# Modulation chunks summed in one PSUM bank per batch, and an eleventh weight block, in a hybrid-then-MoE kernel

## The chip, the core and the metric

The kernel runs on one core of one Trainium2 chip. Its time is device time in microseconds (us), the median of three runs; the profile is one more execution, taken with the hardware profiler. TensorE is called PE in the profile's rows, VectorE DVE, ScalarE ACT, GpSimd POOL and SyncE SP. Nearly all loads are issued from SP's queue, which takes its instructions in order.

## The reference, cut to what matters

A block of two hybrid layers is followed by a block of two layers, each a mixer (neighbourhood attention, then grouped-query attention) and a mixture of 32 experts. All is fp32, with 256 tokens and D = 1024.

```python
c_act = jax.nn.silu(c)                                   # (1, 1024)
for i in range(DEPTH):                                   # 2 layers
    mod = c_act @ ada_w[i] + ada_b[i]                    # (1, 6 * 1024)
    sh1, sc1, g1, sh2, sc2, g2 = jnp.split(mod[:, None, :], 6, axis=-1)
    h = x * (1 + sc1) + sh1
    y = neighbourhood_mixer(h, ...) if i % 2 == 0 else gqa_mixer(h, ...)
    x = layer_norm(ALPHA * x + (1 + g1) * y, ...)
    h = x * (1 + sc2) + sh2
    y = hierarchical_moe(h, ...)   # sum of gate * (silu(h @ w_gate) * (h @ w_up)) @ w_down
    x = layer_norm(ALPHA * x + (1 + g2) * y, ...)
```

The part the change touches is `mod`: a vector of 2 x 6144 numbers from 24 weight chunks of 1024 x 512, of which each is 2 MB. An expert has 6 MB of weights: two gate_up halves and one down matrix of 2 MB each.

## The kernel before

**Weight blocks.** All large weights pass through blocks of 2 MB (`block`, 128 partitions of 16 KB). Eight (0 to 7) exist from the start, 8, 9 and 10 from the end of the hybrid layers on. A list, `ring`, says which block the next load takes: `chunk` pops its first entry and appends it again, so a load waits until the block's former content has been used. In the hybrid layers and the neighbourhood layer the ring is 0, 1, 2, 7; blocks 3 and 4 hold the weights' split into a high and a low part (`splitter`), 5 the transposed input, 6 the attention output, and 8, 9, 10 the queries, keys, values and scores. At an expert stage (`moe`) the ring is lengthened (L991): by 8, 9, 10, 3, 4, 5 in the first stage, by 7, 8, 9, 10, 3, 4, 5 in the second. Between the stages `role` renames the ten blocks in the order in which the first stage lets go of them, and the GQA layer uses 0, 1, 2 as its ring and 7, 9 and then 7, 2 for modulation chunks.

**Order of work.** The kernel is written as one stream of operations over tiles. A scheduler simulates it when the program is built and fixes the order on each engine and on SP's queue: the program's order is a priority, and an operation that is ready in the simulation may pass one that is not.

**Modulation chunks.** `ada_steps` (L724) yields the 24 chunks in two steps each, the load and the use; `ada()` takes as many steps at a place as `ADA_PLAN` (L28) says. So chunks 0 to 7 are loaded in the hybrid layers, 8 to 15 in the neighbourhood layer, 16 to 23 in the GQA layer. 22 chunks go over PE (`ada_cols`, L688): the condition vector stands 32 times side by side as the weight (`cact`), and 16 matmuls of 256 columns work in four groups of 32 PE columns into the one bank with the tag `pf`; the result is copied to `parts`, and a tail, run after the next chunk, turns it into four columns by two matmuls with two columns each (`sel`) and adds the bias into `modc`. Chunks 2 and 10 are stored transposed and go over DVE: four products with the condition row `crow` (L698), each with a sum along the row. The warm-up matmuls (`warm`) use the `pf` bank too.

**An expert stage** takes 16 pairs of experts: for a pair four gate_up loads and two down loads, the matmuls of the hidden layer, those of the down matrix and a scatter into the output that is held in four banks. After pair 8 there is a conditional part for experts with more than 32 tokens.

Of the kernel before, what the change touches and what calls it, by code (L numbers as in the profile page):

```python
# [7 lines left out]
F32 = mybir.dt.float32  # L8
# [3 lines left out]
OP = mybir.AluOpType  # L12
# [5 lines left out]
    0, 128, 256, 384, 768, 792, 824, 952, 956, 964, 966, 973)  # L18
# [8 lines left out]
ADA_ROWS = [int(i) for i in '001000000010000000000000']  # L27
# [4 lines left out]
def tile_hybrid_then_moe(ctx: ExitStack, tc: tile.TileContext, p: dict, out: bass.AP):  # L32
# [65 lines left out]
    def carve(b, *shapes):  # L98
        o, vs = 0, []
        for sh in shapes:  # L100
            n = 1
            for d in sh:
                n *= d
            v = b[:, o:o + n]
            o += n
            names = "abcde"[:len(sh)]
            if len(sh) > 1:
                v = v.rearrange(f"p ({' '.join(names)}) -> p {' '.join(names)}", **dict(zip(names[1:], sh[1:])))
            vs.append(v)
        return vs  # L110
# [41 lines left out]
    sel = cst[:, C_SEL:C_SEL + 2]  # L152
# [76 lines left out]
    def start(tmp):  # L229
# [19 lines left out]
        nc.sync.dma_start(crow, p["c_2"].partition_broadcast(128))  # L249
        th, csil = carve(tmp, (256,), (8,))  # L250
        for i in range(4):
            c = crow[:, i * 256:i * 256 + 256]
            S.activation(th, c, AF.Tanh, scale=0.5)
            V.tensor_scalar(th, th, 0.5, 0.5, op0=OP.mult, op1=OP.add)
            V.tensor_tensor(c, c, th, OP.mult)
# [3 lines left out]
        V.tensor_copy(cact, csil[:, :, None].to_broadcast([128, 8, 32]))  # L259

    cact = const.tile([128, 8, 32], F32, name="cact")
    crow = const.tile([128, D], F32, name="crow")
# [157 lines left out]
    def hybrid(l, w1, split, start=None):  # L420
# [256 lines left out]
        ada()  # L677

# [4 lines left out]
    pend = []  # L683

    def flush():
        while pend:
            pend.pop()()

    def ada_cols(l, sec, c, n):
        b0 = K_ADA + (l * 6 + sec) * 8 + c * 4  # L690
        o, b, one = modc[:, l, sec, c * 4:c * 4 + 4], col[:, b0:b0 + 4], 0.0 if sec in (0, 3) else 1.0
        w = chunk(adab[0] and adab[0]())
        nc.sync.dma_start(w, p["ada_w_2"][n])
        yield
        if ADA_ROWS[n]:
            w = w.rearrange("p (j k) -> p j k", j=4)
            for j in range(4):
                V.scalar_tensor_tensor(w[:, j], w[:, j], 1.0, crow, op0=OP.mult, op1=OP.mult, accum_out=o[:, j:j + 1])  # L698
            V.scalar_tensor_tensor(o, o, one, b, op0=OP.add, op1=OP.add)
            flush()  # L700
            yield
            return
        w = w.rearrange("p (k f) -> p k f", k=8)
        part = parts[:, c * 256:c * 256 + 256]
        first, ps = pin[0], PF()
        for k in range(4):
            for q in range(4):
                kk, f0 = q % 2 * 4 + k, q // 2 * 256
                i = mm(ps[32 * q:32 * q + 32, 0:256], cact[:, kk], w[:, kk, f0:f0 + 256], k == 0, k == 3)
                if first and k == q == 0:  # L710
                    tc.keep_in_program_order(i)
        evac(part, ps[:, 0:256])
        flush()

        def tail():
            ps = PF()
            for i in range(2):
                a = part[:, i * 128:i * 128 + 128]
                mm(ps[:, 2 * i:2 * i + 2], a, sel, True, True)
            V.scalar_tensor_tensor(o.rearrange("p (a i) -> p a i", i=2), ps[:, 0:4].rearrange("p (i a) -> p a i", i=2),  # L720
                                   one, b.rearrange("p (a i) -> p a i", i=2), op0=OP.add, op1=OP.add)

        pend.append(tail)
        yield  # L724

    def ada_steps():
        for n in range(24):
            yield from ada_cols(n // 12, n // 2 % 6, n % 2, n)
# [6 lines left out]
    def ada(n=None):  # L735
        for _ in range(next(plan) if n is None else n):
            next(steps, None)
# [252 lines left out]
    def moe(l, w1, lg, fs, fb, new):  # L990
        ring.extend(new)  # L991
# [263 lines left out]
    blocks(ctx.enter_context(pool("bigB", side="right")), range(8, 11))  # L1255
    w1 = ctx.enter_context(pool("misc"))
    for l in range(2):
        if l == 0:
            nxt = na_layer(l, split)
            adab[0] = None  # L1260
        else:
            role.update(zip((0, 7, 10, 8, 3, 4, 5, 1, 9, 2), ring))
            ring[:] = [0, 1, 2]
            adab[0] = cyc([7, 9])
            split = splitter()
            nxt = gqa_layer(l, split)
        moe(l, w1, *nxt, ([] if l == 0 else [7]) + [8, 9, 10, 3, 4, 5])


def _consts():  # L1270
# [11 lines left out]
    c[:, C_SEL:C_SEL + 2] = (i[:, None] % 32 == 0) & (i[:, None] // 64 == np.arange(2))  # L1282
# [17 lines left out]
def _layout(inp):  # L1300
# [16 lines left out]
    a["c_2"] = np.ascontiguousarray(g["c_2"][0])  # L1317
# [5 lines left out]
    for n in range(24):  # L1323
        l, s, c = n // 12, n // 2 % 6, n % 2
        w = g["ada_w_2"][l, :, s * D + c * 512:s * D + c * 512 + 512]
        if ADA_ROWS[n]:
            w = w.T.reshape(4, 128, D).transpose(1, 0, 2)
        else:
            w = w.reshape(8, 128, 512).transpose(1, 0, 2)
        a["ada_w_2"][n] = w.reshape(128, 4 * D)  # L1330
# [52 lines left out]
```

## Time and profile before

| | us |
|---|---|
| median of three runs | 1541.78 (1540.99 to 1545.21) |
| the profiled execution, its own time | 1540.82 |
| its span, first to last instruction | 1537.7 |
| PE busy | 1221.9 (79%) |
| DVE busy | 585.8 (38%) |
| ACT busy | 355.9 (23%) |

DMA moved 532.75 MB in the span. By the rows, the hybrid layers end at about 309 us, the first expert stage runs from about 480 to 926, the GQA layer from there to about 1083, and the second expert stage to the end. The row groups below are cited by number. A window's row gives the busy time of each engine in that stretch; a waits row says who waited for whom; SP's rows give the time at which loads are issued, not when they land. A matmul on fp32 data stands in the trace as two records.

### The profile page before, as it was taken

The numbers are of one execution on the slowest core, as the hardware profiler recorded it, in microseconds if no ns is written. First come the engines' busy times: TensorE is split into PE (matmuls) and PEld (weight loads), VectorE is DVE, ScalarE is ACT, GpSimd is POOL, SyncE is SP. The second block draws the span as 40 slices with busy tenths as digits, with TensorE's granted clock in tenths as the row PEclk, the third lists the DMA queues.
The fourth block names the chain that finished last, engine by engine and source line by source line (L and its number), as shares of the span: only waits on it lengthen the run. The fifth ranks groups of instructions, "written<-read, shape, count | busy, mean of one in ns | idle before, by whom it ended". The sixth has DMA issues, their size and how long they took to land.

```text
span 1537.7 us, 24637 instructions
## 1 busy us (share of the span) xinstructions
PE 1221.9 (79%) x10584; PEld 788.6 (51%) x10584; DVE 585.8 (38%) x1434; ACT 355.9 (23%) x759; POOL 48.1 (3%) x83
## 2 busy tenths in 40 slices
PE   6999899999998976674976767998897764686775
PEld 6897788787866432322432325757443321233322
DVE  6886687566575210100110116878311100011103
ACT  6454444435441100000100004472000000010000
POOL 0000000000000200000000000000300000000000
PEclk9999899999999998876998888999899877899798
DMA  9546553676487999999999997766999999999995
GB/s 368 192 174 263 219 191 117 262 280 254 183 339 317 425 428 428 426 427 425 427 427 426 427 425 326 291 276 250 378 428 428 427 427 427 426 427 427 427 428 214
DMA packets 46704, 532.75 MB, mean 346 GB/s; under 512 B 7040, under 2 KB 10240, under 8 KB 15104
## 3 DMA queue, kind: packets, MB, share of 16 engines
q1 hardware_dynamic: 45440, 527.99, 83.5%
q10 hardware_dynamic: 1152, 3.15, 0.5%
q8 instruction: 85, 1.39, 0.4%
q14 instruction: 27, 0.22, 0.0%
HBM read 530.07 MB, written 1.05 MB: 345 GB/s over the span
## 4 chain that ended last, share of the span: by engine, by line
DMA 46%; PE 43%; DVE 8%; ACT 2%; issue 1%; SPq 0%; DVEq 0%; ACTq 0%
DMA b<-in_moe_w_gate_up_dram 25%; DMA b<-in_moe_w_down_dram 19%; PE ps L159 13%; PE pd L174 11%; PE ps L174 11%; PE pd L159 3%; PE pf L159 2%; PE ps L156 2%; DVE b L125 2%; DMA b<-in_na_bias_dram 1%; ACT b L124 1%; DMA b<-in_ada_w_dram 1%; DMA b<-in_w_in_dram 0%; DVE b L217 0%; DVE mx L349 0%
## 5 line engine op out<-in xcount | busy, mean ns | idle before, releaser
L159 PE MATMUL ps<-b,b 128*32 128x256 f32 (+2 forms) x5248 | 484.0, 475 | 193.3 <-DMA b<-in_moe_w_gate_up_dram 129.5
L159 PEld LDWEIGHTS ps<-b,b 128*32 128x32 f32 (+1 forms) x5248 | 193.7, 120 | 426.2 <-issue 269.6
L174 PE MATMUL pd<-b,b 128*128 128x256 f32 (+2 forms) x1152 | 189.7, 322 | 8.0 <-DVE b L468 3.9
L174 PE MATMUL ps<-b,b 128*128 128x256 f32 (+1 forms) x1464 | 194.9, 292 | 0.8 <-DVE ch L217 0.5
L174 PEld LDWEIGHTS ps<-b,b 128*128 128x128 f32 x1464 | 183.8, 192 | 9.0 <-issue 3.6
L174 PEld LDWEIGHTS pd<-b,b 128*128 128x128 f32 x1152 | 163.5, 198 | 29.2 <-DVE b L468 5.9
L125 DVE TENSOR_TENSOR b<-b,b 128x1024 fp32r<-128x1024 f32 (+1 forms) x124 | 148.6, 1207 | 65.9 <-ACT b L124 64.6
L124 ACT CAST b<-b 128x1024 fp32r<-128x1024 f32 (+1 forms) x124 | 126.3, 1035 | 156.6 <-PE ps L174 70.0
L223 ACT COPY b<-ps 128x256 f32<-128x256 f32 (+1 forms) x81 | 36.0, 448 | 445.6 <-PE ps L159 298.8
L217 DVE COPY b<-ps 128x256 f32<-128x256 f32 (+1 forms) x71 | 36.0, 507 | 260.6 <-PE ps L159 216.6
L1096 DVE SCALAR_TENSOR_TENSOR sl<-sl,ps 128x128 f32<-128x128 f32 x64 | 18.4, 287 | 231.7 <-ACT sl L1095 231.7
L156 PE MATMUL ps<-cst,b 128*128 128x128 f32 (+1 forms) x404 | 75.3, 293 | 37.4 <-DVE b L217 17.4
L156 PEld LDWEIGHTS ps<-cst,b 128*128 128x128 f32 (+1 forms) x404 | 43.0, 141 | 102.4 <-DVE b L217 34.4
L159 PE MATMUL pd<-b 64*128 64x512 f32 (+1 forms) x384 | 83.1, 551 | 14.6 <-DVE b L1144 11.3
L1144 DVE TENSOR_TENSOR b<-ps,parts 128x512 f32<-128x512 f32 x32 | 22.1, 691 | 174.5 <-PE ps L159 173.7
L159 PEld LDWEIGHTS ps<-b,x 128*128 128x128 f32 x512 | 69.8, 222 | 26.2 <-issue 21.9
L159 PE MATMUL ps<-b,x 128*128 128x128 f32 x512 | 73.6, 309 | 9.2 <-PEq L1168 6.3
L1095 ACT ACTIVATE sl<-ps 128x128 f32<-128x128 f32 x64 | 17.7, 277 | 237.1 <-PE ps L156 237.1
L1114 POOL TENSOR_TENSOR b<-b,g 128x128 f32<-128x128 f32 x64 | 23.5, 399 | 1277.0 <-DVE b L1110 728.4
L159 PEld LDWEIGHTS pd<-b 64*128 64x128 f32 x384 | 34.7, 190 | 52.0 <-issue 24.3
L227 ACT ACTIVATE b<-ps,modc 128x128 f32<-128x128 f32 x64 | 29.0, 457 | 130.7 <-DVE b L221 77.5
L221 DVE TENSOR_SCALAR b<-ps,modc 128x128 f32<-128x128 f32 x64 | 25.8, 408 | 80.1 <-ACT b L227 41.9
(294 smaller groups left out, 855.8 us busy)
## 6 DMA issues: line engine op xcount, KB each, us to landing
b<-in_moe_w_gate_up_dram SPq DMA_DIRECT2D x128, 2048.0 KB, 32.1
b<-in_moe_w_down_dram SPq DMA_DIRECT2D x62, 2048.0 KB, 35.8
b<-in_ada_w_dram SPq DMA_DIRECT2D x24, 2048.0 KB, 8.7
b<-in_w_in_dram SPq DMA_DIRECT2D x12, 2048.0 KB, 8.4
b<-in_na_w_qkv_dram SPq DMA_DIRECT2D x6, 2048.0 KB, 8.1
b<-in_gqa_w_qkv_dram SPq DMA_DIRECT2D x3, 2048.0 KB, 24.0
b<-in_w_out_dram SPq DMA_DIRECT2D x4, 1024.0 KB, 6.8
b<-in_w_out_dram SPq DMA_DIRECT2D x2, 2048.0 KB, 7.5
```

The source lines that it names most:

```text
L124: S.copy(hi[:, s], v[:, s])
L125: V.tensor_tensor(lo[:, s], v[:, s], hi[:, s].bitcast(F32), OP.subtract)
L156: T.transpose(o, a, ident)
L159: return T.matmul(o, lhsT=a, rhs=b, start=start, stop=stop)
L174: T.matmul(o, lhsT=a[u], rhs=b[v], start=start and i == 0, stop=stop and i == 2)
L217: V.tensor_copy(o, i)
L221: V.tensor_scalar(o, i, scale, bias, op0=OP.mult, op1=OP.add)
L223: S.copy(o, i)
L227: S.activation(o, i, AF.Identity, scale=scale, bias=bias)
L1096: V.scalar_tensor_tensor(sl, sl, 1.0, ps[:, 0:128], op0=OP.add, op1=OP.mult)
L1114: G.tensor_tensor(PG[:, t, :, du].rearrange("p q (e s) -> p q e s", e=2), P[:, t].rearrange("p (q e) s -> p q e s", q=2), g32[:, t, 4 * g: ...
L1144: V.tensor_tensor(do, ps, parts, OP.mult)
```

## The change

There are four edits.

1. All 24 chunks go over PE. A chunk is now 8 matmuls of 512 columns (2 times four column groups). The weight is a window of 32 columns in `cz`, whose only column that is not zero stands at place s: so chunk s of a batch adds its result to row s of each group of 32 in one bank that stays open for the batch, and zero to the other rows. A batch ends after chunk 6, 15 and 23. Then `flush` copies the bank to `parts` on DVE and ACT, does four matmuls with a 0/1 matrix of n columns for n chunks, and one addition of the bias. The 1 of `1 + scale` and `1 + gate` is added to the bias columns at the start. `flush` is called at the end of the second hybrid layer and, as before, at the end of both attention layers ahead of the output projection.
2. The condition row (`crow`, 4 KB in each partition) with its load and the operations on it is gone, and the program's transfer scratch is set to 1024 bytes.
3. The room makes block 11, which joins the ring after the hybrid layers, in front. It has the role 11 in the GQA layer, which does not use it.
4. The ring of an expert stage is set anew: in the first stage the ring's three older blocks, then 8, 9, 10, then the two that hold the output projection's weights, then 3, 4, 5; in the second stage block 2, then 11, 7, 8, 9, 10, then 0 and 1 with the output projection's weights, then 3, 4, 5.

```diff
-ADA_ROWS = [int(i) for i in '001000000010000000000000']
+ADA_LAST = (6, 15, 23)
...
-        nc.sync.dma_start(crow, p["c_2"].partition_broadcast(128))
-        th, csil = carve(tmp, (256,), (8,))
-        for i in range(4):
-            c = crow[:, i * 256:i * 256 + 256]
-            S.activation(th, c, AF.Tanh, scale=0.5)
-            V.tensor_scalar(th, th, 0.5, 0.5, op0=OP.mult, op1=OP.add)
-            V.tensor_tensor(c, c, th, OP.mult)
+        csil, = carve(tmp[:, 256:264], (8,))
...
-        V.tensor_copy(cact, csil[:, :, None].to_broadcast([128, 8, 32]))
+        V.memset(cz, 0.0)
+        V.tensor_copy(cz[:, :, 31], csil)
+        b = col[:, K_ADA:K_ADA + 96].rearrange("p (g n) -> p g n", g=4)[:, :, 8:24]
+        V.tensor_scalar(b, b, 1.0, None, op0=OP.add)
...
         ada()
+        if l:
+            flush()
...
-    pend = []
+    batch, held = [], [None]

     def flush():
-        while pend:
-            pend.pop()()
+        if not batch:
+            return
+        n0, n = batch[0], len(batch)
+        assert batch[-1] in ADA_LAST
+        acc, ps = held[0], PS()
+        evac(parts[:, 0:256], acc[:, 0:256], e="v")
+        evac(parts[:, 256:512], acc[:, 256:512], e="s")
+        for i in range(4):
+            mm(ps[:, i * n:(i + 1) * n], parts[:, i * 128:i * 128 + 128], sel[:, 0:n], True, True)
+        o = modc.rearrange("p l s k -> p (l s k)")[:, 4 * n0:4 * (n0 + n)]
+        b = col[:, K_ADA + 4 * n0:K_ADA + 4 * (n0 + n)]
+        V.tensor_tensor(o.rearrange("p (s i) -> p s i", i=4), ps[:, 0:4 * n].rearrange("p (i s) -> p s i", i=4),
+                        b.rearrange("p (s i) -> p s i", i=4), OP.add)
+        batch.clear()
+        held[0] = None
...
-        if ADA_ROWS[n]:
-            w = w.rearrange("p (j k) -> p j k", j=4)
-            for j in range(4):
-                V.scalar_tensor_tensor(w[:, j], w[:, j], 1.0, crow, op0=OP.mult, op1=OP.mult, accum_out=o[:, j:j + 1])
...
-        first, ps = pin[0], PF()
-        for k in range(4):
+        s = len(batch)
+        if not s:
+            held[0] = PF()
+        batch.append(n)
+        for k in range(2):
             for q in range(4):
-                kk, f0 = q % 2 * 4 + k, q // 2 * 256
-                i = mm(ps[32 * q:32 * q + 32, 0:256], cact[:, kk], w[:, kk, f0:f0 + 256], k == 0, k == 3)
+                i = mm(held[0][32 * q:32 * q + 32], cz[:, 4 * k + q, 31 - s:63 - s], w[:, 4 * k + q],
+                       s == 0 and k == 0, n in ADA_LAST and k == 1)
...
-        evac(part, ps[:, 0:256])
-        flush()
-        def tail():
-            ps = PF()
-            for i in range(2):
-                a = part[:, i * 128:i * 128 + 128]
-                mm(ps[:, 2 * i:2 * i + 2], a, sel, True, True)
...
-        ring.extend(new)
+        ring[:] = new
...
-    blocks(ctx.enter_context(pool("bigB", side="right")), range(8, 11))
+    blocks(ctx.enter_context(pool("bigB", side="right")), range(8, 12))
+    ring.insert(0, 11)
...
-            role.update(zip((0, 7, 10, 8, 3, 4, 5, 1, 9, 2), ring))
+            role.update(zip((0, 7, 10, 8, 3, 4, 5, 1, 9, 2, 11), ring))
...
-        moe(l, w1, *nxt, ([] if l == 0 else [7]) + [8, 9, 10, 3, 4, 5])
+        order = ring[:-2] + ([11, 7] if l else []) + [8, 9, 10] + ring[-2:] + [3, 4, 5]
+        moe(l, w1, *nxt, order)
...
-    nc = _bacc.Bacc("TRN2", target_bir_lowering=False, num_devices=1)
+    nc = _bacc.Bacc("TRN2", target_bir_lowering=False, num_devices=1, dynamic_dma_scratch_size=1024)
```

## Rows read from the trace of the kernel before

**Rows 1.** The page, the span in 40 equal slices: DMA busy tenths, bytes moved

```profile
DMA  9546553676487999999999997766999999999995
GB/s 368 192 174 263 219 191 117 262 280 254 183 339 317 425 428 428 426 427 425 427 427 426 427 425 326 291 276 250 378 428 428 427 427 427 426 427 427 427 428 214
```

**Rows 2.** Longest waits of TensorE, 500:925, then 1110:1538: us in total, times, longest

```profile
PE ps L159 <- DMA b<-in_moe_w_gate_up_dram: 63.2, 29, 13.3
...
PE ps L159 <- DMA b<-in_moe_w_gate_up_dram: 66.3, 26, 20.5
```

**Rows 3.** SP's queue in order of time: start us, us it covers, operation, count

```profile
459.71 14.73 SPq L1081 DMA_DIRECT2D b<-in_moe_w_gate_up_dram  x4
488.60 2.05 SPq L1081 DMA_DIRECT2D b<-in_moe_w_down_dram  x2
...
797.01 15.09 SPq L1081 DMA_DIRECT2D b<-in_moe_w_gate_up_dram  x4
...
990.68 0.33 SPq L1081 DMA_DIRECT2D b<-in_moe_w_gate_up_dram  x1
...
1005.43 11.22 SPq L1081 DMA_DIRECT2D b<-in_moe_w_gate_up_dram  x2
1024.84 17.78 SPq L1081 DMA_DIRECT2D b<-in_moe_w_down_dram  x2
1042.71 27.86 SPq L1081 DMA_DIRECT2D b<-in_moe_w_gate_up_dram  x5
1085.88 2.05 SPq L1081 DMA_DIRECT2D b<-in_moe_w_down_dram  x2
```

**Rows 4.** Windows: busy us of PE, PEld, DVE, ACT, POOL; PEclk, DMA, GB/s

```profile
345.00:420.00 75.00, 70.48 (x596) 60.09 (x594) 44.91 (x73) 34.19 (x70) 0.00 (x0) 0.98 0.57 211
420.00:445.00 25.00, 22.80 (x164) 13.77 (x164) 14.25 (x38) 14.27 (x48) 0.00 (x0) 1.00 0.96 393
445.00:465.00 20.00, 17.72 (x88) 13.83 (x85) 17.38 (x36) 5.98 (x8) 0.00 (x0) 1.00 0.77 289
465.00:500.00 35.00, 31.14 (x305) 23.60 (x306) 19.38 (x81) 6.03 (x14) 1.47 (x4) 0.95 0.79 315
...
945.00:990.00 45.00, 45.00 (x428) 40.72 (x431) 32.02 (x82) 19.94 (x26) 0.00 (x0) 1.00 0.62 246
...
1030.00:1060.00 30.00, 27.50 (x138) 19.98 (x137) 19.35 (x38) 10.28 (x21) 0.00 (x0) 1.00 0.53 200
1060.00:1085.00 25.00, 22.17 (x167) 20.48 (x169) 17.78 (x78) 5.44 (x13) 1.47 (x4) 0.86 0.72 292
```

**Rows 5.** DMA in 1060:1090, 40 slices of 0.75 us

```profile
GB/s 415 502 371 22 0 0 22 0 0 0 284 66 240 459 393 393 481 415 437 393 459 437 437 393 437 437 481 393 437 437 415 66 0 22 0 186 197 175 481 350
```

**Rows 6.** Groups of 0:470, then 925:1060: busy us, mean ns, idle before by cause

```profile
L159 PE MATMUL pf<-b,cact 128*32 128x256 f32 x448 | 33.9, 392 | 2.1 <-DMA b<-in_ada_w_dram 1.3 <-DVE parts L217 0.5 <-DVE modc L720 0.3
...
L698 DVE SCALAR_TENSOR_TENSOR b<-b,crow 128x1024 f32<-128x1024 f32 x8 | 9.4, 1218 | 0.3 <-issue 0.3
...
L159 PE MATMUL pf<-cst,parts 128*128 128x2 f32 x56 | 7.7, 241 | 4.0 <-DVE parts L217 3.1 <-ACT parts L223 0.7 <-DVE modc L720 0.2
...
L159 PE MATMUL pf<-b,cact 128*32 128x256 f32 x256 | 17.6, 398 | 3.6 <-DMA b<-in_ada_w_dram 2.2 <-DVE modc L720 1.4
...
L159 PE MATMUL pf<-cst,parts 128*128 128x2 f32 x32 | 4.4, 243 | 0.2 <-DVE parts L217 0.2
```

**Rows 7.** The page, DMA queues: packets, MB, share of 16 engines

```profile
q1 hardware_dynamic: 45440, 527.99, 83.5%
q10 hardware_dynamic: 1152, 3.15, 0.5%
```

**Rows 8.** Bias loads, 355:360, then 410:440: us from issue to landing; who waited

```profile
DMA to landing us min/median/max: 7.4/7.5/7.6
...
  DVE b L877: 5.0, 2
...
DMA to landing us min/median/max: 11.4/13.7/16.1
```

## What the change does to the time: the prediction

> **What bounds the kernel now.** I read the page's slices first. The DMA line stands at 9 and the bytes line at 425 to 428 GB/s in slices 13 to 23 and 29 to 38 (counted from 0, 38.4 us each) [rows 1]: these are the two expert stages, and they run at the speed at which weights arrive. The waits of TensorE confirm it: in each expert stage its longest wait by far is for a gate_up load, 63.2 and 66.3 us in total [rows 2]. One block is 2 MB; the queue issues four of them in 15.09 us, which is three intervals and an issue of 0.33, so (15.09 - 0.33) / 3 = 4.92 us for a block [rows 3]. Outside those stages DMA is not the limit. The windows before the first expert stage and in the GQA layer show TensorE busy for 70.48 of 75 us, 22.80 of 25, 45.00 of 45 and 27.50 of 30, while DMA moves only 211 to 393 GB/s [rows 4]. So there are two prices: in an expert stage a saved TensorE or VectorE microsecond is worth nothing, and a block that is already in SBUF when the stage begins is worth 4.92 us; everywhere else TensorE time counts and bytes do not.
>
> What sets an expert stage's start? Before it, the queue fetches expert weights into blocks as these fall free, and then it stops because no block is left. At the second stage ten loads go out between 990.68 and about 1070.6 (990.68, two from 1005.43, two from 1024.84, five from 1042.71), and the next one at 1085.88, when expert 0 has given back its first block [rows 3]. The bytes line of 1060 to 1090 has two holes in it, seven slices of 0 or 22 from 1062 to 1067 and three around 1085 [rows 5]. The first stage has the same shape: the four loads from 459.71 end the filling, and the next load is at 488.60 [rows 3]. From there on DMA has no hole until the last expert. So the end of each stage is this restart, plus the blocks still to come times 4.92, plus a tail that does not change.
>
> **The change part by part.**
>
> *The eleventh block.* With eleven blocks the restart finds eleven loaded and one less to come: 4.92 us at each stage, provided that the extra load fits ahead of the restart. Bytes at 427 GB/s that were not moved give the room: (427 - 211) / 427 x 75 = 37.9 us in 345 to 420, 2.0 in 420 to 445, 6.5 in 445 to 465, 9.2 in 465 to 500; in the second stage 19.1 us in 945 to 990, 15.9 in 1030 to 1060 and 7.9 in 1060 to 1085 [rows 4]. One load needs 4.92. In the second stage block 11 is idle through the whole GQA layer, since no role of that layer uses it, so its load can go out as soon as the last expert of the first stage has let go of it. In the first stage the ring of five has to hand back its blocks in time: the last five modulation chunks and the two output-projection loads take places 7, 11, 0, 1, 2, 7, 11, so experts begin in 0, 1, 2 behind chunks 13 to 15 and not, as now, in two blocks behind chunks 14 and 15 and two that wait for the output projection's split. Blocks 3, 4 and 5 fall free last, as now, at the end of the output projection; the three loads into them are late in both versions, and the eight others have all of 345 to 470 to land. I take the full 4.92 twice, 9.8 us; the ends are 0 (the load stands behind something and comes after the restart) and 9.8. The restart itself waits on TensorE's use of expert 0 and not on DMA, so it does not move later with a fuller ring.
>
> *The new order of blocks.* The order in which SP issues is not the program's: the program asks for four gate_up loads before the first two down loads, and in the second stage the two go out in the row at 1024.84, behind only three [rows 3]. So a block that falls free early is already used early, and the order by itself adds nothing to the eleventh block: 0. It cannot cost in the stage, where every block is filled anyway.
>
> *Modulation chunks on TensorE.* Now a chunk is 32 records, 448 for 14 chunks, 33.9 us, and 17.6 us for the 8 of the GQA layer: 2.42 and 2.20 us each. A tail is four records of 0.24 us on a 128x128 weight: 7.7 us for 14, 4.4 us for 8 [rows 6]. After, a chunk is 8 matmuls of 512 columns in place of 16 of 256: the same columns through the same four column groups, so I take the same time. All 22 tails go (12.1 us), and with them the waits for the chunk's read-out: 4.0 and 0.2 us ahead of the tails' matmuls, and of the main matmuls' waits the part not due to a load, 0.8 and 1.4 us [rows 6]: 6.4 us. Two chunks come over from VectorE: 2 x 2.42 = 4.8 us. Three flushes of four matmuls each, twice a tail's 0.55 us: 3.3 us. Sum: 12.1 + 6.4 - 4.8 - 3.3 = 10.4 us less TensorE time, 5.5 of it before the first expert stage, 4.9 in the GQA layer, none in the expert stages. TensorE is busy for 142 of the 155 us from 345 to 500 and for 95 of the 100 us of the GQA windows [rows 4], so some of the gap that opens will be taken back by the splits and softmaxes that it then waits for. The ends are 0 and 10.4; I take 6, nearer to the upper end because the windows are nearly full.
>
> *What leaves VectorE, ScalarE and the queue.* The row chunks take 9.4 us of VectorE [rows 6]; 22 read-outs of 128x256 become three of 128x512, shared by both engines; the condition row takes a 512 KB load and twelve small operations with it. In windows where TensorE is this full the other engines' work lies beside it, so 0; it is the margin behind taking 6 above. The added memset, one copy and the added 1 on the bias columns are three small operations at the start: 0.
>
> *Where new waits are.* The bank is held from a batch's first chunk to its flush, so the next batch's first chunk and the warm-up matmuls, which use the same bank, queue behind the flush. Batch 0 ends with chunk 6 ahead of the neighbourhood layer, whose feed reads its columns; batch 1 and 2 end ahead of each output projection, whose fold reads them. Each flush is a read-out, four matmuls and an addition; the wait of one such read-out is part of the 4.0 us for 14 tails above. If all three stood open on TensorE they would cost about what six or seven tails wait now, 2 us. The feed of the neighbourhood layer is the only reader that can stand directly behind one; what the folds make is read at the end of the output projection, by the logits. I take 0, with 2 as the other end.
>
> *The transfer scratch.* It shrinks from its default to 1 KB. Every byte of this kernel goes over the hardware queues, 527.99 and 3.15 MB, or is instructions [rows 7]. I take 0. The Trainium skill (SBUF — State Buffer, "SBUF size: 192, 224, or 256?") says that this scratch holds the descriptor ring of software-generated DMAs; by that page too the sum has 0 here, and no run shows it yet.
>
> The sum: -4.9 - 4.9 - 6 = -15.8 us. The profiled execution takes 1540.8 us (span 1537.7), which is 1.0 us under the median of the runs; 1541.8 - 15.8 = 1526 us.
>
> **The rivals.** *Blocks alone.* What TensorE saves is handed back to VectorE and ScalarE, which feed it. For it: the windows leave TensorE 5 to 13 us in which it waits for exactly these engines [rows 4]. Then 9.8 us: 1532. *More than the sum.* The bias loads of the neighbourhood layer take 7.5 us when the queue is empty (357 to 360) and up to 16.1 us at 416, where expert and output-projection loads have just gone out, and VectorE waits 5.0 us for them [rows 8]. With five blocks the second output-projection load goes out before that point. If these 5.0 come back and TensorE gives all 10.4: 1541.8 - 9.8 - 10.4 - 5.0 = 1516.6. *It does not do what it says.* The load of block 11 is put behind modulation loads that wait, or a smaller scratch hinders loads, and the restart finds ten blocks; then only part of the 6 is left, about 1538. *Slower.* The same collision with the other sign: more blocks are free in the neighbourhood layer, so expert loads stand in the queue through all of its second half. Six of the eight bias loads are issued after 355; the first two of these took 7.4 and 7.6 us, the last two 11.4 and 16.1 [rows 8]. Were all six at 16.1, that is 6 x 8.6 less what the last two already pay (3.9 + 8.6), 39 us; the two buffers hide some of it, and with two thirds showing (my estimate) 27: 1526 + 27 = 1553. It decides from the point where three 2 MB loads are in flight at each of those issues; against it, only one more block (behind chunk 13) falls free for experts before the splits of the second half's weights are through. In the Trainium skill (DMA: Bandwidth & Descriptors, "Queues, rings and completion order") each DMA engine takes packets from its queues in turn, by which a bias load could at most take about twice its time alone however deep the other queue is; the 16.1 us against 7.5 us agree with that, and by it this rival would stop at its price here.
>
> **How the numbers follow.** Forecast 0.55; blocks alone 0.15; more 0.13; not as it says 0.08; slower 0.09. A measurement of this kernel tells about 0.3% (4.6 us) from no change. Everything under 1537.2 us is faster by more: the first three and about a third of the fourth, 0.86; the rest of the fourth and a slice of the last, within 0.3%: 0.06; slower 0.08. The range of 1511 to 1538 takes in the bounds of all costs but the slower case.
>
> **What would show it.** In the profile after: eleven expert loads ahead of the restart in each stage; the restart about 5 us earlier at the first stage, and the saturated stretch to the last load one block shorter in both; no 2-column matmuls but in three places; no VectorE operations of 1.2 us from the condition row. It would be wrong if expert loads fill the queue at the bias loads, if a flush stands in front of the feed, or if the GQA layer keeps its length while its tails are gone.

## The result and the profile after

The changed kernel takes 1524.8 us (median of four runs, 1522.76 to 1528.28) against 1542.42 (1540.99 to 1545.21) for the kernel before on the same chip: a ratio of 0.988, 95% interval 0.9865 to 0.9894. The forecast of 1526.0 is 1.2 us off. The profiled execution is the slowest of the four, 1528.28 us with a span of 1526.4; the other three span 1519.7 to 1523.5.

The page's slices, DMA busy and bytes, answer to [rows 1]:

```profile
DMA  9538444768477999999999999775999999999995
GB/s 360 219 124 336 173 157 159 297 259 349 184 282 291 429 430 430 429 429 430 430 429 430 430 428 381 280 276 212 378 428 431 428 429 430 430 428 430 430 430 211
```

The stages are as full as before, but at 428 to 431 GB/s where [rows 1] have 425 to 428. Nothing in the prediction asked for that.

SP's queue, answering to [rows 3] (start us, us that the row covers, operation, count):

```profile
457.67 11.93 SPq L1072 DMA_DIRECT2D b<-in_moe_w_gate_up_dram  x3
472.08 16.01 SPq L1072 DMA_DIRECT2D b<-in_moe_w_down_dram  x2
...
917.08 0.33 SPq L1072 DMA_DIRECT2D b<-in_moe_w_gate_up_dram  x1
...
980.54 0.33 SPq L1072 DMA_DIRECT2D b<-in_moe_w_gate_up_dram  x1
...
1004.34 13.38 SPq L1072 DMA_DIRECT2D b<-in_moe_w_gate_up_dram  x3
1032.28 0.80 SPq L1072 DMA_DIRECT2D b<-in_moe_w_down_dram  x2
1049.63 13.84 SPq L1072 DMA_DIRECT2D b<-in_moe_w_gate_up_dram  x3
1065.95 16.03 SPq L1072 DMA_DIRECT2D b<-in_moe_w_down_dram  x2
```

Eleven loads now stand ahead of the second restart: 1, 1, 3, 2, 3 and the first of the last two; the second of these is issued at its row's end less 0.33, at 1081.65, and is the restart. The first goes out at 917.08 already, where it was 990.68 before [rows 3]. The first restart is the second of the two at 472.08, by the same working at 487.75, against 488.60 before.

Windows of TensorE's two full stretches, answering to [rows 4] (same columns):

```profile
345.00:420.00 75.00, 68.69 (x541) 53.18 (x539) 43.33 (x67) 34.85 (x80) 0.00 (x0) 0.99 0.66 263
...
945.00:990.00 45.00, 40.29 (x313) 32.40 (x315) 38.13 (x102) 21.45 (x33) 0.00 (x0) 0.91 0.71 273
```

In the second, TensorE was busy for all 45 us at a granted clock of 1.00; now for 40.29 at a mean of 0.91. Part of that is a shift, since the first stage now ends 7.3 us earlier: at the same place of the kernel before (952.3 to 997.3) TensorE was busy for 43.31 us, at 1.00.

The chunks' groups of 0:500, then 905:1085, answering to [rows 6]:

```profile
L159 PE MATMUL pf<-b,cz 128*32 128x512 f32 x256 | 34.9, 599 | 2.0 <-DMA b<-in_ada_w_dram 2.0
...
L159 PE MATMUL ps<-cst,parts 128*128 128x9 f32 x8 | 1.1, 260 | 0.0
L159 PE MATMUL ps<-cst,parts 128*128 128x7 f32 x8 | 1.0, 245 | 0.0
...
L159 PE MATMUL pf<-b,cz 128*32 128x512 f32 x128 | 19.1, 661 | 1.8 <-DMA b<-in_ada_w_dram 1.8
...
L159 PE MATMUL ps<-cst,parts 128*128 128x8 f32 x8 | 1.2, 261 | 0.0
```

The tails of [rows 6] and their waits for a read-out are gone, and the three flushes cost TensorE 1.1, 1.0 and 1.2 us. Its busy time over the span fell from 1221.9 to 1213.0 us.

To see where the time went I cut each trace at five events: the last addition to x in the hybrid layers, the first restart, the landing of the first stage's last expert load, the second restart, and the end. All tables below have these stretches (differences of two event times, one profiled execution of each kernel; hence the executions' scatter of a few us is in them).

| us | hybrid layers | neighbourhood layer | rest of stage 1 | GQA layer | rest of stage 2 | span |
|---|---|---|---|---|---|---|
| before | 308.4 | 180.2 | 431.1 | 166.2 | 451.8 | 1537.7 |
| after | 307.7 | 180.1 | 424.7 | 169.2 | 444.8 | 1526.4 |
| difference | -0.7 | -0.1 | -6.4 | +3.0 | -7.0 | -11.2 |

In these two executions all of the gain, 13.4 us, lies in the two expert stages, where 9.8 were forecast. The layers, where 6 were forecast, gave back 2.2. The table accounts for 11.2 us, though, while the medians differ by 17.6: the traced execution of the kernel before lies 1.6 us under its median, that of the changed kernel 3.5 us over it. The stages hardly scatter: together they take 882.9 us here and 883.2 in another trace with ten blocks and the old chunks, and 868.1 to 869.5 in six traces with eleven blocks and the new chunks. If the untraced executions are no different there, the layers gave some 4 us by the medians (my estimate, 17.6 - 13.4), and no trace shows where. So the sum was right and its terms were not, and the experiments are about that: what is the eleventh block worth, why do the stages gain more than it, and what eats TensorE's 8.9 us?

### The profile page after: what moved, and what is told of

The parts are those of the page before. It is cut to its first block, busy times and chain, and to the rows that moved or that the text cites. A ratio compares the mean times of both kernels' runs of the same rounds, so it can differ in the third digit from the quotient of the medians.

```text
span 1526.4 us, 23782 instructions
## 1 busy us (share of the span) xinstructions
PE 1213.0 (79%) x10200; PEld 763.6 (50%) x10200; DVE 576.3 (38%) x1383; ACT 352.5 (23%) x747; POOL 47.9 (3%) x83
## 4 chain that ended last, share of the span: by engine, by line
DMA 46%; PE 43%; DVE 7%; ACT 3%; issue 1%; SPq 0%; DVEq 0%; ACTq 0%
DMA b<-in_moe_w_gate_up_dram 27%; DMA b<-in_moe_w_down_dram 17%; PE ps L159 13%; PE ps L174 11%; PE pd L174 11%; PE pd L159 3%; PE pf L159 3%; PE ps L156 2%; DVE b L125 2%; DMA b<-in_na_bias_dram 1%; ACT b L356 1%; ACT b L124 1%; DMA b<-in_w_in_dram 1%; DVE diag L744 0%; DVE b L868 0%
## 5 line engine op out<-in xcount | busy, mean ns | idle before, releaser
L174 PE MATMUL ps<-b,b 128*128 128x256 f32 (+1 forms) x1464 | 195.4, 293 | 1.5 <-DVE b L125 1.3
L174 PE MATMUL pd<-b,b 128*128 128x256 f32 (+2 forms) x1152 | 188.0, 321 | 5.7 <-DVE b L464 4.0
L174 PEld LDWEIGHTS ps<-b,b 128*128 128x128 f32 x1464 | 183.9, 192 | 12.1 <-issue 3.2
L174 PEld LDWEIGHTS pd<-b,b 128*128 128x128 f32 x1152 | 163.4, 197 | 31.5 <-issue 7.1
L159 PEld LDWEIGHTS ps<-b,x 128*128 128x128 f32 x512 | 62.8, 202 | 20.8 <-issue 15.7
L159 PE MATMUL ps<-b,x 128*128 128x128 f32 x512 | 67.1, 290 | 3.7 <-DVE b L1101 1.6
L159 PE MATMUL pf<-b,cz 128*32 128x512 f32 x384 | 54.0, 620 | 3.7 <-DMA b<-in_ada_w_dram 3.7
```

What stands on the lines that cost most here:

```text
L159: return T.matmul(o, lhsT=a, rhs=b, start=start, stop=stop)
L174: T.matmul(o, lhsT=a[u], rhs=b[v], start=start and i == 0, stop=stop and i == 2)
```

## The experiments

**1. The parts alone.** Three kernels. The first is the kernel before with the transfer scratch alone:

```diff
-    nc = _bacc.Bacc("TRN2", target_bir_lowering=False, num_devices=1)
+    nc = _bacc.Bacc("TRN2", target_bir_lowering=False, num_devices=1, dynamic_dma_scratch_size=1024)
```

> The kernel before with the transfer scratch set to 1024 bytes and nothing else. Theories 1 and 2: no difference, ratio 1.000 with 427 GB/s in the expert stages. Theory 3 (the rate depends on the scratch): 430 GB/s and 5.6 us less, ratio 0.9964.

Measured: a ratio of 1.0004 (0.9992 to 1.0016). No cost and no gain of the scratch can be measured.

The second has block 11, its role and the new order, on the kernel before with its chunks as they were; room for it is found by a still smaller scratch (256):

```diff
-    blocks(ctx.enter_context(pool("bigB", side="right")), range(8, 11))
+    blocks(ctx.enter_context(pool("bigB", side="right")), range(8, 12))
+    ring.insert(0, 11)
...
-        moe(l, w1, *nxt, ([] if l == 0 else [7]) + [8, 9, 10, 3, 4, 5])
+        order = ring[:-2] + ([11, 7] if l else []) + [8, 9, 10] + ring[-2:] + [3, 4, 5]
+        moe(l, w1, *nxt, order)
```

> The kernel before, with block 11, the new rings and a transfer scratch of 256 bytes; the chunks work as before. Theory 1 (a block ahead of each restart is the whole gain): 11 expert loads ahead of the restart in both stages, 9.8 us less than before, ratio 0.9936. Theory 2 (the TensorE edits give some 6 us as well): the same here, 0.9936. Theory 3 (the smaller scratch lets loads run faster, 430 GB/s in place of 427): 9.8 and another 0.65% of the 855 us of saturated loading, 5.6 us: ratio 0.990, with 430 GB/s in the expert stages.

The third is the changed kernel with ten blocks and the rings of before, so the chunks alone:

```diff
-    blocks(ctx.enter_context(pool("bigB", side="right")), range(8, 12))
-    ring.insert(0, 11)
+    blocks(ctx.enter_context(pool("bigB", side="right")), range(8, 11))
...
+        moe(l, w1, *nxt, ring + ([] if l == 0 else [7]) + [8, 9, 10, 3, 4, 5])
```

> The changed kernel with ten blocks, the old rings and the default scratch: the edits to the modulation chunks alone. Theory 1 (what TensorE saves is handed back in the layers): within 2 us of before, ratio 0.999 to 1.001, first restart less than 2 us earlier, GQA layer not shorter. Theory 2 (the step of the prediction): 6 us less, ratio 0.996, first restart 3 us earlier and the GQA layer 3 us shorter. Theory 3: nothing, 427 GB/s.

Measured: blocks alone 0.9943 (0.9928 to 0.9958), chunks alone 0.9985 (0.9973 to 0.9997).

| us | hybrid | neighbourhood | stage 1 | GQA | stage 2 | loads before the restarts |
|---|---|---|---|---|---|---|
| before | 308.4 | 180.2 | 431.1 | 166.2 | 451.8 | 10, 10 |
| blocks alone | 307.6 | 187.3 | 426.4 | 165.1 | 447.8 | 11, 11 |
| chunks alone | 306.7 | 187.4 | 429.8 | 167.3 | 448.8 | 10, 10 |
| after | 307.7 | 180.1 | 424.7 | 169.2 | 444.8 | 11, 11 |

The eleventh block takes 4.7 and 4.0 us off the stages, 8.7 where 9.8 was forecast: this step holds. The loads of blocks alone run at 426.7 and 426.9 GB/s in the two stages, so a smaller scratch does not make them faster. Two things were not forecast. Chunks without a new block also shorten the stages, by 1.3 and 3.0 us. And each part alone makes the neighbourhood layer 7 us longer, which the whole change does not.

**2. The order of blocks.** The changed kernel with the block order of before:

```diff
-        order = ring[:-2] + ([11, 7] if l else []) + [8, 9, 10] + ring[-2:] + [3, 4, 5]
+        order = ring + ([11, 7] if l else []) + [8, 9, 10, 3, 4, 5]
```

> The changed kernel with eleven blocks, but the expert rings in the old manner: the layer's ring first, with the output projection's two blocks, and only then 8, 9, 10, 3, 4, 5. Prediction's step (the order adds nothing, since SP's order lets a load pass one that waits): as the changed kernel, ratio 0.988 against before. Rival (the order is what lets the eleventh block be filled in the first stage): 10 loads ahead of the first restart and 4.9 us back, ratio 0.991; if both stages depend on it, 9.8 us back, 0.994.

Measured: 0.9889 (0.987 to 0.9908), eleven loads ahead of each restart, stages of 423.8 and 445.0 us. The order adds nothing that can be told from the scatter, as forecast. The GQA layer of this trace takes 166.1 us, though, and not 169.2; experiment 5 comes back to that.

**3. What makes the loads faster.** The candidates were the condition row, no longer in DRAM among the inputs, and the place of the blocks in SBUF: the condition row's 4096 bytes a partition are gone, `cz` is 992 larger than `cact` was and the constants 120, so all that lies behind moves by about 3 KB. One kernel has the chunks alone and keeps the condition row as an input that nobody reads, the other fills the gap in SBUF (one execution each):

```diff
+    a["c_2"] = np.ascontiguousarray(g["c_2"][0])
```

> chunks_only with the condition row put back as an input in device memory that nothing reads. In chunks_only the expert stages load at 429.7 GB/s, in the kernel before, blocks_only and scratch_only at 426.7 to 427.0. Theory 5 (the place of the weights in device memory): back at 427 GB/s. Theory 6 (the place of the blocks in SBUF): still 429.7 GB/s.

```diff
     cz = const.tile([128, 8, 63], F32, name="cz")
+    pad = const.tile([128, 744], F32, name="pad")
+    V.memset(pad[:, 0:1], 0.0)
```

> chunks_only with an unused tile of 744 numbers in each partition, which puts every weight block back at the SBUF address that it had before. Theory 6 (the place of the blocks in SBUF sets the rate): back at 427 GB/s in the expert stages. Theory 5 (device memory): still 429.7 GB/s.

Windows inside the two expert stages, first with the padding:

```profile
560.00:860.00 300.00, 206.22 (x1958) 96.76 (x1950) 35.65 (x93) 20.58 (x56) 9.59 (x23) 0.84 1.01 427
1150.00:1480.00 330.00, 223.70 (x2184) 104.66 (x2175) 39.83 (x103) 23.59 (x64) 9.59 (x23) 0.87 1.01 427
```

and with the input kept:

```profile
560.00:860.00 300.00, 203.24 (x1952) 93.90 (x1942) 35.65 (x93) 20.55 (x56) 9.56 (x23) 0.85 1.01 430
1150.00:1480.00 330.00, 230.87 (x2236) 108.68 (x2229) 39.81 (x103) 24.19 (x66) 9.56 (x23) 0.85 1.01 430
```

The last column decides. With the padding the rate is that of before, 427 (426.9 and 427.1 by the trace's bytes); with the input kept it stays at 430 (429.8, 429.9). The stretches follow: 432.3 and 452.1 us with the padding, 429.8 and 448.8 without, so the place is worth 2.6 and 3.3 us, together 5.9 (against the kernel before, chunks alone gain 4.3 in the stages). The place in SBUF sets the rate; why 3 KB do so, no run tells.

**4. The 7 us of the neighbourhood layer.** In the traces so far a layer of 180 us went with the fourth bias load of the layer landing 57.1 to 61.0 us after the hybrid layers, one of 187 us with 64.6 (chunks alone) and 67.7 (blocks alone). With chunks alone three 2 MB loads are in flight when it is issued, and it takes 13.7 us; in the kernel before it is one, and 7.4 us. This looks like the mechanism of the rival on the slower side. The first try was to keep block 11 out of the layer's ring and hand it to the stage alone, on the changed kernel and on blocks alone:

```diff
-    ring.insert(0, 11)
...
-        order = ring[:-2] + ([11, 7] if l else []) + [8, 9, 10] + ring[-2:] + [3, 4, 5]
+        order = ring[:-2] + ([11, 7] if l else [11]) + [8, 9, 10] + ring[-2:] + [3, 4, 5]
```

> The changed kernel, but block 11 joins only at the expert stage: the neighbourhood layer keeps the ring of four. Theory 4 (the chunk edits lengthen the neighbourhood layer when its ring has four blocks, as in chunks_only, and the fifth block takes that back): first restart at about 494 us, 6 us later than in the changed kernel, still 11 loads ahead of it, ratio 0.992 against before. Rival (the length of that layer follows from the fixed order as a whole and not from the fifth block): first restart anywhere from 487 to 494 us, ratio 0.988 if near 488.

> blocks_only, but block 11 joins only at the expert stage, so the neighbourhood layer has its old ring of four and its old chunks. Theory 4 (old chunks and ring of four fit each other, 180 us from the end of the hybrid layers to the restart; old chunks with a ring of five take 187): first restart back at 488 to 489 us with 11 loads ahead of it, 6 us less than blocks_only, ratio 0.990 against before. Rival: it stays at 494 us, ratio 0.994.

Measured: 0.9947 (0.9926 to 0.9968) on the changed kernel, where 0.992 was expected; its layer goes from 180.1 to 187.1 us, as expected. On blocks alone 0.9945 (0.9925 to 0.9966), and its layer stays at 187.0, against what was expected. So the fifth block in the ring does not make the long layer. With the new chunks it takes the 7 us back; without them, taking it out does not help. It does not do so by sparing the fourth bias load: that takes 13.4 us in the changed kernel too, with three 2 MB loads in flight, but is issued 47.7 us after the hybrid layers, and 50.9 without the fifth block.

The second try takes away what makes the load late: it waits for one of two buffers. Chunks alone with four buffers, and (with `range(1)`) the changed kernel with three, where a scratch of 256 bytes gives the room:

```diff
-        ebs, bufs = cyc([e0, e1]), (cyc([s0, s1]), cyc([t0, t1]))
+        more = [w1.tile([128, 2, 384], F32, name="eb%d" % i, tag="eb%d" % i) for i in range(2)]
+        ebs, bufs = cyc([e0, e1] + more), (cyc([s0, s1]), cyc([t0, t1]))
```

> The chunks on TensorE without the eleventh block, with four buffers in place of two for the bias loads of the neighbourhood layer. Theory (the long neighbourhood layer comes from bias loads that are issued late, because a buffer is still in use, and then lie beside 2 MB loads): with two more buffers the fourth bias load is issued before the 2 MB loads; the neighbourhood layer goes from 187 us to 181 or less, the first restart comes at about 488 us, and the ratio to the kernel before falls from 0.9985 to about 0.9945. Rival (the 7 us come from the order that was fixed for the engines when the program was built, and the bias load is late because its consumer is): the layer stays at 187 us, the restart at 494, the ratio at 0.9985.

> The changed kernel with three buffers in place of two for the bias loads of the neighbourhood layer. Theory (bias loads that wait for a buffer still cost the changed kernel something, since VectorE waits 5.9 us for them): the layer goes from 180 us to 176 to 178, the ratio from 0.988 to 0.985 or 0.986. Rival (these waits lie beside TensorE's work, or the order moves against it): the layer stays at 180 us or grows, and the ratio at 0.988 or above.

The bias loads of the layer, chunks alone (issue to landing; who waited for them, us and times):

```profile
  DVE b L868: 5.1, 2
...
DMA to landing us min/median/max: 3.3/10.8/15.7
```

With four buffers the view has no waiter left. The layer falls from 187.4 to 182.1 us, the first restart from 494.0 to 488.7, the ratio from 0.9985 to 0.9948 (0.9928 to 0.9968). The changed kernel with three buffers loses its own waits, 5.9 us on VectorE; its layer goes from 180.1 to 176.9, and the ratio is 0.9872 (0.9852 to 0.9893), which the measurement can't tell from 0.988.

So more buffers give back 5.3 us. They do not show that bias loads make the 7 us. The two waits that vanish, 2.0 and 3.1 us for the last two bias loads, stand in the kernel before as well, with 2.2 and 2.8, and its layer takes 180.2. The chain of waits (start us, us, piece) has another load between 350 and 400 us. First chunks alone, then the kernel before, then blocks alone:

```profile
352.67 18.41 DMA b<-in_ada_w_dram
```

```profile
355.80 8.32 DMA b<-in_ada_w_dram
```

```profile
359.63 15.65 DMA b<-in_na_bias_dram
```

With chunks alone it is a modulation load, issued as the third of three 2 MB loads; it lands 64.4 us after the hybrid layers, where the one of the kernel before lands after 55.7. With blocks alone it is the fourth bias load. In the changed kernel no load stands in the chain there. With four buffers the same modulation load still takes 17.4 us, but the order of the engines is another one and the load is not in the chain. So each part alone meets a late load of its own, and only that of blocks alone is the rival's. How these loads add up to 7 us was not measured, and the kernel before was not run with more buffers.

**5. The GQA layer's lost gain.** VectorE and ScalarE prepare the last query heads while TensorE has little to do. Windows of the changed kernel there, and the chunk matmuls that follow (start us, us, operation, count):

```profile
976.50:990.00 13.50, 8.79 (x53) 5.62 (x55) 12.31 (x35) 8.50 (x18) 0.00 (x0) 0.71 0.59 203
990.00:1004.00 14.00, 13.33 (x88) 5.33 (x80) 11.13 (x22) 9.31 (x31) 0.00 (x0) 0.91 0.85 321
```

```profile
988.77 5.47 PE L159 MATMUL pf<-b,cz 128*32 128x512 f32 x26
```

The same work of the kernel before, which still has tails and smaller chunk matmuls there:

```profile
986.60:1000.00 13.40, 10.69 (x118) 7.16 (x117) 12.24 (x34) 8.92 (x21) 0.00 (x0) 1.00 0.63 245
```

TensorE sat idle for 4.7 of 13.5 us, and the granted clock fell to a mean of 0.71, that is partly to the lower level of 1.2 GHz. 26 records take 5.47 us; elsewhere 16 take 1.92. To test whether this costs the layer its gain, eight matmuls of 128 columns were put into the gap:

```diff
+        def keep(v):
+            ps = PS()
+            for _ in range(4):
+                mm(ps[:, 0:128].rearrange("p (h d) -> p h d", h=2), ones, v, True, True)
...
+            if busy:
+                keep(q[:, 0, 0:2])
...
+                if busy and t == 0:
+                    keep(qk_t[:, 0, 0:2])
```

> The changed kernel with eight extra matmuls of 128 columns on the data of the last query chain of the GQA layer, whose results nobody reads; nothing is left out. Theory (the removed chunk tails and waits left a stretch at 977 to 990 us in which TensorE is idle for some 5 us, the granted clock falls to 0.71 there, and the chunk and attention matmuls behind it run at half rate): the granted clock stays near 1.0 from 976 to 1004 us, the 26 chunk records at 988 us take about 3 us in place of 5.5, the GQA layer takes about 166 us in place of 169, the ratio goes from 0.988 to about 0.986. Rival (the extra matmuls stand in front of the layer's own, or the layer waits for VectorE there anyway): the layer stays at 169 us or grows, the ratio at 0.988 or above, whatever the clock does.

Windows of this kernel, shifted by 3.9 us, since its first stage ends so much earlier:

```profile
972.60:986.10 13.50, 10.35 (x81) 7.02 (x79) 12.21 (x33) 8.25 (x17) 0.00 (x0) 1.00 0.48 169
986.10:1000.10 14.00, 11.04 (x68) 5.35 (x70) 11.06 (x24) 9.76 (x32) 0.00 (x0) 0.88 0.94 356
```

```profile
983.80 2.76 PE L159 MATMUL pf<-b,cz 128*32 128x512 f32 x18
```

The clock is back at 1.00 in the first window, and 18 chunk records take 2.76 us, but TensorE is then idle in the next window instead (busy for 11.04 of 14 us, 13.33 in the changed kernel), the layer takes 170.4 us and the ratio is 0.9895 (0.9877 to 0.9913). So a full clock in this stretch brought the layer nothing. Whether the added matmuls took something themselves can't be told from this kernel.

The chain of waits shows the place. It follows the work that ended last back to its causes (start us, us, piece, number of instructions). In the kernel before, from the last head's matmuls to the output projection (`pd L174`):

```profile
1039.99 2.66 PE ps L159 x14
1042.67 0.29 DVE diag L744
1042.96 0.33 DVE b L846
1043.29 0.60 DVE b L217
1043.89 0.39 DVE diag L744 x2
1044.42 0.61 DVE b L805
1045.08 3.06 PE pd L174 x12
...
1059.62 2.77 PE ps L174 x12
```

In the changed kernel:

```profile
1030.01 2.75 PE ps L159 x16
1032.78 0.19 DVE modc L695
...
1033.84 0.42 DVE parts L775
1034.34 0.39 DVE diag L735 x2
1034.73 0.57 DVE parts L776
1035.30 0.37 DVE b L775
...
1036.71 1.78 PE ps L159 x6
1038.49 3.67 PE pd L174 x12
...
1053.79 4.34 PE ps L174 x12
```

From the first line to the output projection it is 1045.08 - 1039.99 = 5.09 us before and 1038.49 - 1030.01 = 8.48 after (8.49 with the old block order). In between stands the flush's addition (L695), and behind it the fold that the output projection needs (L735, L775, L776). The kernel before had done part of it ahead, as soon as the tails of those chunks were through: its counterparts of L775 and L776 stand in its chain at 1020.96 to 1022.7. The read-out of the flush is done at 1013; its matmuls come at 1030.58, in the order that was fixed when the program was built, among the last head's. Behind it the clock is lower too: twelve matmuls take 3.67 and 4.34 us where before they took 3.06 and 2.77. The last kernel therefore writes the last chunks and the flush behind the fifth head pair, with three bias buffers as above:

```diff
-        adab[0] = cyc([7, 2])
-        ada(48)
-        flush()
+            if hp == 4:
+                adab[0] = cyc([7, 2])
+                ada(48)
+                flush()
```

> The changed kernel with three buffers for the bias loads of the neighbourhood layer and, in the GQA layer, the last chunks and the flush written behind the fifth of eight head pairs instead of behind the eighth; nothing is left out. Theory (the flush stands on the path: its read-out is done at 1013 us in the changed kernel, but its four matmuls come at 1030.6 to 1032.7 among the last head's, then the addition and the fold, so that the output projection's first matmul comes 5.7 us after the read of the last flush matmul, where the kernel before took 2.4): the fold is done before the last head, the chain from the last attention matmul to the output projection is 3 us shorter, the GQA layer goes from 169 us to 165.5 or 166, the neighbourhood layer stays at 177, and the ratio goes from 0.987 to about 0.985. Rival (TensorE is idle for longer or at a lower clock there anyway, so that what the flush gives is taken back): the GQA layer stays at 168 to 170 us and the ratio at 0.987.

Its chain at the same place:

```profile
1026.32 2.66 PE ps L159 x14
1029.01 0.29 DVE diag L735
1029.29 0.33 DVE b L837
1029.62 0.60 DVE b L217
1030.22 0.39 DVE diag L735 x2
1030.75 0.61 DVE b L796
1031.41 3.07 PE pd L174 x12
```

1031.41 - 1026.32 = 5.09 us, as before the change. The GQA layer takes 166.7 us (169.1 with three buffers alone), the neighbourhood layer 175.5. The median is 1520.59 us (1518.82 to 1524.12), the ratio 0.9859 (0.9833 to 0.9885): the fastest kernel of this study, 22 us under the kernel before. Its interval and that of the changed kernel overlap, so that the last 3 or 4 us rest on the stretches and the chain, not on the medians.

The late flush is not all that the layer lost, as its pieces show (us; from the end of the first stage's loads to the last head's last matmul, from there to the output projection, from its first record to its thirteenth, and the rest to the restart):

| us | to the last head | to the projection | its first twelve records | rest | GQA layer | granted clock in these twelve |
|---|---|---|---|---|---|---|
| before | 122.5 | 2.9 | 3.0 | 37.8 | 166.2 | 1.00 |
| after | 119.8 | 5.9 | 4.0 | 39.5 | 169.2 | 0.73 |
| old order | 118.7 | 6.0 | 4.9 | 36.6 | 166.1 | 0.58 |
| three bias buffers | 120.2 | 5.9 | 5.2 | 37.8 | 169.1 | 0.53 |
| with the early flush | 122.9 | 2.9 | 3.0 | 37.9 | 166.7 | 1.00 |

Up to the last head the changed kernel is 2.8 us ahead of the kernel before. The flush takes 3.1 of that back, and the lower clock behind it 2.7 more in this execution. With the early flush both losses are gone, and so is the lead; why the stretch ahead grew by as much was not tested. So the GQA layer is no shorter than before even in the last kernel. How much of such differences is scatter two kernels show that do the same work, chunks alone and the same with the input that nobody reads: their GQA layers take 167.3 and 164.3 us.

## Why the prediction was right, and where its steps were not

*What bounds the kernel* holds. Both stages run from the restart at the speed of the loads, and TensorE's longest wait in them is still for a gate_up load, 63.8 and 63.3 us, as in [rows 2].

*The eleventh block* is the step that carries the result: forecast 9.8 us, measured 8.7 alone. The room for it was there, as [rows 4] said. That the restart would come about 5 us earlier at the first stage was wrong: 0.85 us, since it waits for TensorE's use of expert 0 at the end of the neighbourhood layer, and that layer did not get shorter.

*Modulation chunks on TensorE* is the step that failed. The work itself was sized well: 10.4 us less were forecast, and TensorE's busy time fell by 8.9, with flushes of 1.0 to 1.2 us each. But "I take 6, nearer to the upper end because the windows are nearly full" does not hold in the traces: there the layers gave nothing (-0.7, -0.1 and +3.0 us), and even the estimate from the medians, 4 us, leaves their gain under 6. A window in which TensorE is busy for 94% of the time (70.48 of 75 us [rows 4]) says that it is the fullest engine, not that each of its instructions stands on the path. In the neighbourhood layer VectorE then waited for bias loads, 5.0 us before [rows 8] and 5.9 after. Without these waits the layer takes 176.9 and 175.5 us, 3.3 and 4.7 less than before. Whether that is TensorE's saving or only the waits, which the kernel before has too, can't be told: more buffers were not tried on it. In the GQA layer the saving is there up to the last head, 2.8 us of the 4.9 forecast, and is gone behind it.

*Where new waits are* is the second miss, and it is a misreading of the code. I let the feed be "the only reader that can stand directly behind" a flush and took 0, with 2 as the end. In the GQA layer the fold stands behind the last flush and costs 3.4 us by the chain (3.1 from the last head's end), more than the upper end. In the neighbourhood layer the same stretch grew from 3.3 to 3.8 us. The tails of before let each chunk's columns go to their reader as soon as they were done; a batch gives all its columns at its last chunk, and its readers then run one behind the other.

*The transfer scratch* and *the new order of blocks* were taken at 0 and measured at 1.0004, and at 0.9889 beside 0.988.

What made up for the failed 6 us was not in the sum: the loads' rate, 4.3 us in the two stages against the kernel before and 5.9 against the padded one. It came from tiles that shrank, not from the block. That the forecast came out only 1.2 us off is therefore luck: an error in the stages and one in the layers have opposite signs, and the reasons behind the number deserve less trust than the number.

*The rivals.* Blocks alone (1532) gave the right fate to TensorE's gain, and with the rate's 4.3 to 5.9 us it gives 1526 to 1528, near the time measured. More than the sum (1516.6) named bias waits that are real, but the change did not bring them back; with these and the late flush out of the way the last kernel comes to 1520.6. The rival that it does not do what it says fell: there are eleven loads at both restarts. The slower rival's collision stands in the chain of blocks alone; its price does not. The neighbourhood layer is 7 us longer in six kernels that have one part of the change or most of it, not by the 27 that were worked out (two thirds of its 39 are 26), and no longer in the whole. For its bound I had used a rule of the Trainium skill (DMA: Bandwidth & Descriptors, "Queues, rings and completion order"): each DMA engine takes packets from its queues in turn, from which I concluded that a bias load takes at most twice its time alone. The runs don't bear this conclusion out: the same load takes 3.3 us with a quiet queue and 15.7 beside 2 MB loads, nearly five times. The 7.5 us that the prediction called "when the queue is empty" were already disturbed.

The parts don't add up: blocks alone take 0.57% off, chunks alone 0.15%, the whole 1.2%. The gains in the stages do add up, 8.7 and 4.3 to 13.4 within the scatter; what does not is the neighbourhood layer, 7 us longer with each part alone and not with both.

## What to carry to other kernels

An engine that is 94% busy in a layer still need not set the layer's length: before its saved work is counted as time, follow the chain of waits through the stretch and see which of the removed instructions stand in it. When results that were handed over one by one are batched, look for the earliest reader of each, and write the read-out where the last of the batch is done, not where the next step begins. And a change that resizes a small constant tile moves all that lies behind it, so test its parts with and without padding before the gain is given to the part that was meant to bring it.

## What the runs showed of the hardware

- The rate of 2 MB loads into SBUF depended on where the blocks lay: 426.6 to 427.1 GB/s in five kernels with the old place, 429.3 to 429.9 in nine with one some 3 KB lower in each partition; 2976 bytes of padding are what puts one of the five back at 427. In the two stages this is 5.9 us against the padded kernel. Which property of the address it is stays open.
- A bias load (128 partitions of 3 KB) took 3.3 us with a quiet queue and 8.5 to 17.1 us in all traces with two or three 2 MB loads of the other queue in flight when it was issued.
- In a stretch of the changed kernel in which TensorE waited for other engines for 4.7 of 13.5 us, the granted clock fell to 0.71 on average, and the matmuls behind it took 5.47 us for 26 records, where elsewhere 16 took 1.92. With eight matmuls of no use in that stretch the clock was 1.00, and the kernel was no faster.
